# Attention scores q k^T: another order of the 32 KB pieces in the large loads, and of the heads on TensorE

## The chip, the cores and the metric

The kernel runs on one core of a Trainium2 chip. The metric is the device time of one execution in microseconds (us), as the median of several runs. A core has a matrix engine (PE, or TensorE), three engines for elementwise work (DVE or VectorE, ACT or ScalarE, POOL or GpSimd), SP, which here only issues DMAs, and sixteen DMA engines that move data between the memory outside the core (DRAM, here HBM) and the on-chip memory (SBUF, 128 partitions). PE writes into PSUM, a small memory of its own, from which ACT or DVE copies.

## The reference

For each of 8 x 12 = 96 heads the kernel computes the 1024 x 1024 matrix of dot products of the rows of q with the rows of k, over 64 elements, in float32.

```python
batch, n_heads, seq, head_dim = 8, 12, 1024, 64
def reference(q, k):
    return np.einsum('bhid,bhjd->bhij', q, k).astype(np.float32)
```

The inputs are 25.2 MB each, the output is 402.65 MB.

## The kernel before

**Blocks.** The 96 heads are worked in nine blocks of 2, 2, 4, 8 and then five times 16 heads (`sizes`, `NMAX` is 16). For each block, q and k are loaded, cast to fp16, transposed so that the 64 elements of a row lie along partitions, and then multiplied head by head. Two blocks (i and i+1) have their transposed q and k in SBUF at a time (`qk_sb[i % 2]`): block i is multiplied while block i+1 is loaded, cast and transposed. Blocks 0 and 1 go another way (transposed by PE, `cast_rows` and `transpose_rows`), which the change does not touch.

**The load** (`Block.load`, L152 to L164). A block of N heads is one stretch of DRAM. It is cut into 128 equal consecutive pieces, and piece p goes to partition p of `x_sb` as one row. For N = 16 a piece is 32 KB, 128 rows of 64 float32, an eighth of a head, and the load has 4 MB. The 128 partitions are dealt to the sixteen DMA engines, eight to each: by the words of the change, partition 8e+b to engine e as its packet b. So engine e reads the sixteenth of the block that is head e, and at any moment the sixteen engines are 256 KB apart. In block 3 (N = 8) the pieces have 16 KB and the engines are 128 KB apart, in block 2 (N = 4) 8 KB and 64 KB.

There is one raw buffer of 32 KB per partition, so from block 4 on (`i > EARLY`) the load of k waits until q's last cast, and the next q until k's last. The loads of the blocks of 16 are issued from ACT's queue by `next_load(act)`, at heads 1 and 7 of the block before; for block 4 it is head 1 of block 2 and head 2 of block 3 (`LOADS`). All stores are issued from SP's queue.

**Casts and transposes.** `cast_quads` (L200, casts at L210) runs on POOL: it takes a chunk of 32 partitions of raw float32 and writes it as fp16 into one quadrant of a half buffer. Four casts make one chunk, of which each block of 16 has eight: q or k, part 0 or 1, and two halves of the rows (`chunks`). Part 0 takes the partitions 0 to 31 and 64 to 95, part 1 the others, so that in the half buffer the lower 64 partitions hold the two halves of 32 elements of each row from raw partitions below 64, and the upper 64 those from above. `transpose_quads` (L221 to L235) then has DVE transpose the chunk in squares of 32 x 32, which puts the 64 elements of a row along 64 partitions, and its output pattern puts each row at its place in the head. Heads whose raw rows lay in partitions 0 to 63 end in the lower 64 partitions of `qk`, that is in the lower half of PE's rows, the others in the upper half. There are three half buffers. The eight chunks of block i+1 are transposed at the heads `TURNS` of block i, or spread evenly in the first blocks.

**The scores** (`Block.scores`, L255). For head n, `half` says in which half of PE it lies and `g` at which place there. Each head has eight weight loads (L308) and sixteen matmuls of 512 columns (L311). ACT copies PSUM to one of three output buffers (`o_sb`, L288), and SP stores each finished head with one DMA of 4 MB (L301): row 8p+t of the head comes from partition p, so each partition's 32 KB are consecutive in DRAM, and each DMA engine writes 256 KB in a row. Heads are stored in their own order.

**What sets the order of work.** The order on each engine is written out by hand: the loop in `block` calls `scores` for each head, and inside it, after the first or second group of matmuls of a head, the transposes and loads that are due at that head. Head 0 of a block waits for all transposes of the block (`self.ready`); the first copy of a head waits until the store three heads before has left its buffer.

## Time and profile before

| | |
|---|---|
| Runs of the kernel before, median (lowest to highest of 3) | 1062.69 us (1061.64 to 1063.31) |
| The profiled execution | 1062.84 us |
| its span, first to last instruction | 1061.0 us |
| granted TensorE clock | 1.000 |
| busy PE, ACT, DVE, POOL | 700.2, 697.1, 431.0, 354.2 us |
| moved by DMA | 453.21 MB, 427 GB/s over the span |
| HBM read, written | 50.33 MB, 402.65 MB |
| a store of 4 MB, issue to landing, median of 96 | 21.8 us |
| a load of 4 MB, issue to landing, median of five of q, five of k | 24.1, 24.3 us |

How to read it: the profile is of one execution, taken on the chip. "Busy" is the time in which an engine worked. The page cuts the span into 40 slices; its DMA row gives the busy share of the sixteen DMA engines in tenths, 9 standing for 90% or more, and the row below it the rate. For each DMA queue it gives packets, megabytes, and the time of the packets as a share of sixteen engines over the span; since packets overlap a little at their ends, a share over a short window can exceed 100%. A group row gives line, engine, operation, output and input, how many, then busy time, mean ns of one, and the idle time of the engine just before them with what ended most of it. A row for one line gives the shortest, median and longest duration in ns instead. The chain is the work that ended last, followed back step by step to what released it; its rows are start, length, and what ran. Beside its views, the trace holds a record of each DMA packet: start, length, bytes and queue, but not which of the sixteen engines moved it.

### The profile page before, as it was taken

To read this page: it belongs to the slowest core of one execution; us is meant where nothing else is said; L and a number is where in the kernel's file an instruction comes from. 1 tells how busy PE (TensorE), PEld (TensorE's weight loads), DVE (VectorE), ACT (ScalarE), POOL (GpSimd) and SP (SyncE) were. 2 spreads that over 40 slices of the span, in tenths; PEclk is the share of its full clock that TensorE was granted. 3 is DMA by queue.
4 is the path that set the end of the run, shared out by engine and by line. 5 is a ranking of instruction groups with operands and counts; after the bars stand their busy time and mean duration, and the time that the engine had idled before them with its cause. 6 is when DMAs were issued, how large, how long until landed. Compare 5 with 4: busy or idle time off the path is not lost.

```text
span 1061.0 us, 3307 instructions
## 1 busy us (share of the span) xinstructions
PE 700.2 (66%) x1568; PEld 127.3 (12%) x800; DVE 431.0 (41%) x55; ACT 697.1 (66%) x386; POOL 354.2 (33%) x206
## 2 busy tenths in 40 slices
PE   6876744957477748567765856775584777778770
PEld 1111100111011101011111101111110111111110
DVE  2995939029193009339003907600761920000000
ACT  4766655857477747567756756775675777777771
POOL 7927465056380028064006509100913700000000
DMA  9999999999999999999999999999999999999997
GB/s 376 434 435 435 434 434 434 416 421 432 431 434 434 435 429 428 426 435 432 432 422 434 435 427 433 433 434 423 433 429 432 435 434 431 434 434 431 432 431 322
DMA packets 17009, 453.21 MB, mean 427 GB/s; under 512 B 1888, under 2 KB 1888, under 8 KB 2912
## 3 DMA queue, kind: packets, MB, share of 16 engines
q1 hardware_dynamic: 14976, 410.00, 89.7%
q10 hardware_dynamic: 2016, 42.99, 9.8%
q8 instruction: 9, 0.15, 0.0%
q14 instruction: 8, 0.07, 0.0%
HBM read 50.33 MB, written 402.65 MB: 427 GB/s over the span
## 4 chain that ended last, share of the span: by engine, by line
DMA 65%; ACT 16%; PE 7%; DVE 5%; POOL 4%; issue 1%; ACTq 0%; SPq 0%
DMA out_dram<-o_sb 60%; ACT o_sb L288 16%; PE ps_all L311 7%; DVE kT L229 4%; POOL half L210 3%; DMA x_sb<-in_k_dram 2%; DMA x_sb<-in_q_dram 2%; DVE qT L229 1%; DMA o_sb<-in_q_dram 0%; PE ps_all L243 0%; POOL qT L181 0%; DVE kT L250 0%; ACT kT L250 0%; ACTq L36 0%; SPq L169 0%
## 5 line engine op out<-in xcount | busy, mean ns | idle before, releaser
L288 ACT COPY o_sb<-ps_all 128x2048 f32<-128x2048 f32 (+1 forms) x384 | 694.8, 1859 | 333.5 <-DMA out_dram<-o_sb 290.2
L311 PE MATMUL ps_all<-kT,qT 64*128 64x512 f16 x1536 | 696.1, 617 | 328.6 <-ACT o_sb L288 312.8
L210 POOL CAST half<-x_sb 32x2048 f16<-32x2048 f32 x176 | 332.3, 1888 | 482.1 <-DMA x_sb<-in_q_dram 302.2
L229 DVE STREAM_TRANSPOSE qT<-half 128x2048 f16<-128x2048 f16 x22 | 202.6, 9478 | 268.1 <-POOL half L210 268.1
L229 DVE STREAM_TRANSPOSE kT<-half 128x2048 f16<-128x2048 f16 x22 | 202.5, 9539 | 137.5 <-POOL half L210 137.5
L308 PEld LDWEIGHTS <-qT 64*128 64x128 f16 x768 | 124.2, 162 | 897.4 <-issue 878.0
L229 DVE STREAM_TRANSPOSE kT<-kT 128x1024 f16<-128x1024 f16 x2 | 9.4, 4870 | 0.0
L229 DVE STREAM_TRANSPOSE qT<-qT 128x1024 f16<-128x1024 f16 x2 | 9.2, 4780 | 0.0
L210 POOL CAST qT<-o_sb 32x1024 f16<-32x1024 f32 x8 | 8.3, 1035 | 1.2 <-DMA o_sb<-in_q_dram 0.8
L210 POOL CAST kT<-o_sb 32x1024 f16<-32x1024 f32 x8 | 8.3, 1035 | 0.5
L250 DVE COPY qT<-ps_all 128x1024 f16<-128x1024 f16 x2 | 2.4, 1224 | 11.1 <-PE ps_all L243 11.1
L288 DVE COPY o_sb<-ps_all 128x1024 f32<-128x1024 f32 x4 | 4.9, 1225 | 4.4 <-PE ps_all L311 4.4
L243 PE MATMUL ps_all<-ident,qT 128*128 128x128 f16 x16 | 2.1, 311 | 6.8 <-POOL qT L181 6.7
L250 ACT COPY kT<-ps_all 128x1024 f16<-128x1024 f16 x1 | 1.0, 1012 | 4.8 <-PE ps_all L243 4.8
L181 POOL CAST qT<-o_sb 128x512 f16<-128x512 f32 x4 | 2.3, 615 | 3.7 <-DMA o_sb<-in_q_dram 3.7
L250 ACT ACT_TABLE_LOAD x1 | 1.3, 1283 | 2.8 <-issue 2.8
L250 DVE COPY kT<-ps_all 128x1024 f16<-128x1024 f16 x1 | 1.2, 1225 | 4.4 <-PE ps_all L243 4.4
L243 PE MATMUL ps_all<-ident,kT 128*128 128x128 f16 x16 | 2.0, 305 | 0.7 <-ACT o_sb L288 0.7
L181 POOL CAST kT<-o_sb 128x512 f16<-128x512 f32 x4 | 2.4, 618 | 0.3 <-DMA o_sb<-in_q_dram 0.3
L243 PEld LDWEIGHTS ps_all<-ident,qT 128*128 128x128 f16 x16 | 1.5, 141 | 7.1 <-POOL qT L181 7.1
L243 PEld LDWEIGHTS ps_all<-ident,kT 128*128 128x128 f16 x16 | 1.5, 136 | 3.3 <-POOL qT L210 1.6
L359 POOL MEMSET ident<- 128x128 f16 x1 | 0.2, 205 | 0.5 <-SPq L98 0.5
(5 smaller groups left out, 0.7 us busy)
## 6 DMA issues: line engine op xcount, KB each, us to landing
out_dram<-o_sb SPq DMA_DIRECT2D x96, 4096.0 KB, 21.8
x_sb<-in_q_dram ACTq DMA_DIRECT2D x5, 4096.0 KB, 24.1
x_sb<-in_k_dram ACTq DMA_DIRECT2D x5, 4096.0 KB, 24.3
x_sb<-in_q_dram SPq DMA_DIRECT2D x1, 2048.0 KB, 14.6
x_sb<-in_k_dram SPq DMA_DIRECT2D x1, 2048.0 KB, 19.5
o_sb<-in_k_dram ACTq DMA_DIRECT2D x4, 256.0 KB, 4.8
o_sb<-in_q_dram SPq DMA_DIRECT2D x4, 256.0 KB, 5.1
o_sb<-in_q_dram SPq DMA_DIRECT2D x1, 1024.0 KB, 8.2
```

Source lines behind the costliest of these rows:

```text
L181: lambda: nc.gpsimd.tensor_copy(out=rows[:, :, h], in_=self.raw[x][:, h * n : (h + 1) * n].rearrange("p (r d) -> p r d", d=D),),
L210: lambda: nc.gpsimd.tensor_copy(out=dst[q0 : q0 + 32].rearrange("p (r d) -> p r d", d=32), in_=raw[32 * b : 32 * b + 32, c * m : (c + 1) * ...
L229: lambda: nc.vector.transpose(out=dst, in_=buf.rearrange("p (r i) -> p r i", i=32)),
L243: lambda: nc.tensor.transpose(t_ps[:, t], rows[:, t], ident),
L250: lambda: copy(out=dst, in_=t_ps.rearrange("c t m -> c m t")), [done]
L288: lambda: (nc.vector.tensor_copy if by_dve else nc.scalar.copy)(out=dst, in_=ps[:, : w * S]),
L308: return nc.tensor.ldweights(stationary, tile_position=(at, 0))
L311: return nc.tensor.add_instruction(mybir.InstMatmult(name=nc.get_next_instruction_name(), ins=[nc.tensor.lower_ap(moving), nc.tensor.lower ...
L359: cleared = gps.run(lambda: nc.gpsimd.memset(ident, 0.0))
```

## The change

The five blocks of 16 heads (`spread`) are cut into the same 128 pieces of 32 KB, but partition 8e+b now receives piece 16b+e, where it received piece 8e+b. So packet b of the sixteen engines covers 512 KB in a row, two heads. A head's eight pieces are now in eight engines' packets of one number b: head 2b lies in the partitions with e below 8, that is 0 to 63, and head 2b+1 in the upper ones. Therefore the output pattern of the DVE transpose places column e and b separately (it has one more dimension), and in `scores` even heads lie in the lower, odd heads in the upper half of PE, where the first eight heads lay in the lower and the last eight in the upper half. Loads of the smaller blocks, stores, casts, copies and the order of instructions on each engine and queue stay.

```diff
+            self.spread = N == NMAX
...
-            dma = eng.eng.dma_start(
-                out=self.raw[x], in_=src.rearrange("(p r) d -> p (r d)", p=P)
-            )
+            if self.spread:
+                src = src.rearrange("(b e r) d -> e b (r d)", b=NT, e=P // NT)
+            else:
+                src = src.rearrange("(p r) d -> p (r d)", p=P)
+            dma = eng.eng.dma_start(out=self.raw[x], in_=src)
...
-            dst = self.qk[x][:, part * n : (part + 1) * n].rearrange(
-                "c (i r) -> c r i", i=32
-            )[:, c * m : (c + 1) * m]
+            if self.spread:
+                dst = self.qk[x].rearrange("c (b q e r) -> c q r e b", b=NT, q=2, e=4)
+                dst = dst[:, part, c * m : (c + 1) * m]
+                src = buf.rearrange("p (r e b) -> p r e b", e=4, b=NT)
+            else:
+                dst = self.qk[x][:, part * n : (part + 1) * n]
+                dst = dst.rearrange("c (i r) -> c r i", i=32)[:, c * m : (c + 1) * m]
+                src = buf.rearrange("p (r i) -> p r i", i=32)
...
-                lambda: nc.vector.transpose(
-                    out=dst, in_=buf.rearrange("p (r i) -> p r i", i=32)
-                ),
+                lambda: nc.vector.transpose(out=dst, in_=src),
...
-            half, g = divmod(n, self.N // 2)
+            if self.spread:
+                g, half = divmod(n, 2)
+            else:
+                half, g = divmod(n, self.N // 2)
```

## The prediction

> **What bounds the kernel now.** I read the page first: slices, DMA queues, chain, groups.

> ```profile
> DMA  9999999999999999999999999999999999999997
> GB/s 376 434 435 435 434 434 434 416 421 432 431 434 434 435 429 428 426 435 432 432 422 434 435 427 433 433 434 423 433 429 432 435 434 431 434 434 431 432 431 322
> ...
> q1 hardware_dynamic: 14976, 410.00, 89.7%
> q10 hardware_dynamic: 2016, 42.99, 9.8%
> ...
> DMA out_dram<-o_sb 60%; ACT o_sb L288 16%; PE ps_all L311 7%; DVE kT L229 4%; POOL half L210 3%; DMA x_sb<-in_k_dram 2%; DMA x_sb<-in_q_dram 2%; DVE qT L229 1%; DMA o_sb<-in_q_dram 0%; PE ps_all L243 0%; POOL qT L181 0%; DVE kT L250 0%; ACT kT L250 0%; ACTq L36 0%; SPq L169 0%
> ...
> L288 ACT COPY o_sb<-ps_all 128x2048 f32<-128x2048 f32 (+1 forms) x384 | 694.8, 1859 | 333.5 <-DMA out_dram<-o_sb 290.2
> L311 PE MATMUL ps_all<-kT,qT 64*128 64x512 f16 x1536 | 696.1, 617 | 328.6 <-ACT o_sb L288 312.8
> L229 DVE STREAM_TRANSPOSE kT<-half 128x2048 f16<-128x2048 f16 x22 | 202.5, 9539 | 137.5 <-POOL half L210 137.5
> ```

> The DMA engines are never free. ACT idles 290.2 us for o_sb to be stored, PE idles 312.8 us for ACT, and the sum of engine idle time in the trace's DMA packet records, between 5 and 1050 us, is 0.09 us per engine. So the end is a sum of packet times, and a faster compute engine buys nothing. Queue q1 holds the stores, q10 the loads. The dips in GB/s (416, 421, 422, 423) fall in slices with a big load.

> The load packets cost a little more per byte. q1: 0.897 x 1061.0 x 16 / 410.00 = 37.1 us of one engine per MB; q10: 0.098 x 1061.0 x 16 / 42.99 = 38.7. The difference, 1.56 x 42.99 / 16, is 4.2 us per engine. The packet records are sharper: the 1280 32 KB packets of the ten big loads last 1.2536 us in the mean against a median of 1.213, so 80 packets per engine x 0.0406 = **3.25 us**. That is all that a better read order can win in the mean.

> Next, where it is lost: the DMA view of two 4 us windows in the load that runs from 201.8 to 222.5 us, first 206 to 210, then 212 to 216 (packets, MB, share of 16 engines).

> ```profile
> q1 hardware_dynamic: 27, 0.88, 51.2%
> q10 hardware_dynamic: 24, 0.79, 45.5%
> ```

> ```profile
> q10 hardware_dynamic: 31, 1.02, 74.0%
> q1 hardware_dynamic: 30, 0.56, 32.4%
> ```

> In the first, half of the engines read and half write: 0.455 x 64 / 24 = 1.213 us a load packet. In the second, one store has run out, the next has just begun, most engines read at once, and a load packet takes 0.740 x 64 / 31 = 1.53 us. The records show the same in six other big loads: up to 2.3 us a packet in one to four microseconds around the handover of two stores, 1.213 elsewhere. Sixteen engines reading at once are not slow as such: from 13.0 to 16.6 us nothing but block 3's load runs, whose engines stand 128 KB apart (8 pieces of 16 KB):

> ```profile
> q1 hardware_dynamic: 97, 1.57, 102.5%
> ```

> 1.025 x 57.6 / 96 = 0.615 us for 16 KB (one of the 97 is a semaphore write); the fastest such packet took 0.611. The big loads stand 256 KB apart.

> **The change, part by part.** No instruction is added, removed or moved: five loads of q and five of k (the four smaller ones on SP's queue stay as they are), the same 160 big casts and 40 transposes of the five 16-head blocks, the same order on every engine and queue.

> *The read order.* At any moment the sixteen engines now read neighbouring 32 KB pieces, 512 KB in a row, instead of sixteen places 256 KB apart. The packets keep their 32 KB and their partitions, so nothing changes on the SBUF side. The trace has no packet at 32 KB pitch. Bounds from the nearest rows: the 128 KB row (0.615 against 0.611, 0.6%) leaves 80 x 1.213 x 0.006 = 0.6 us of the 3.25; the first load's 1.213 leaves nothing; the worst load's mean (1.3125 us, that of 201.8 us) would cost 80 x (1.3125 - 1.2536) = 4.7 us more than now. I take the 128 KB row, as the only one with sixteen readers and no writer, so the bursts go.

> [...]

> But not the mean engine ends the kernel. Each store ends with one 4-byte semaphore packet per engine; the median of the last sixteen starts at 1054.28 us, the last at 1059.28. One engine falls behind by 0.069 us per store in the 74 store intervals without a big load (the median engine by 0.002). So I count on the last landing. Over the ten stretches of 2 or 3 stores with a load, it took 3.38 us more than its packets at 1.2103 us each (their start-to-start time in undisturbed stretches); the median engine 3.69. Of the 3.38, the same drift in the 21 stores is 1.45 and, if reads drift too, in 80 load packets 0.69. So the gain on the path lies between 1.24 and 3.38 us. The ends are about equally far from what the rows say, since the last engine need not be the same one throughout; I take the middle, **-2.3 us**.

> *The transposes.* The output pattern becomes four-dimensional: 64 by 4 by 8 elements, with steps of 256 and 2048 bytes where one run of 32 had 256.

> ```profile
> L229 DVE STREAM_TRANSPOSE qT<-half x22: 9323/9512/9561, 46.1 to 777.4; 128x2048 f16<-128x2048 f16 x22
> L229 DVE STREAM_TRANSPOSE kT<-half x22: 9311/9588/9689, 64.5 to 846.7; 128x2048 f16<-128x2048 f16 x22
> L229 DVE STREAM_TRANSPOSE qT<-qT x2: 4695/4780/4865, 28.3 to 32.6; 128x1024 f16<-128x1024 f16 x2
> ```

> These rows hold steps of 64 bytes (the 1024-element form), 128 and 256, all at 4.6 to 4.7 ns per element; so I take no change. It could be dearer: no row has two inner steps. The cover is thin in one place, the chain of waits from 118 to 188 us:

> ```profile
> 118.08 23.96 DMA x_sb<-in_k_dram
> ...
> 149.85 36.75 DVE kT L229 x4
> 186.60 0.05 issue
> 186.65 1.94 PE ps_all L311 x4
> ```

> Block 4's k load, four casts, four transposes, then PE and ACT, and the store of head 16 is issued at 196.08, when the fastest engine runs out of stores at 197.2. So at most 1.1 us of delay is hidden there, 0.28 us or 3% per transpose; what is above that goes to the end four times over. The later blocks end their transposes (at 327.6 us the first) tens of microseconds before they are used.

> *The head order.* 80 heads alternate between the halves of PE. If each lost the overlap of its first weight load, 80 x 0.16 us = 13 us would lie on PE, inside the 312.8 us it waits for ACT. A longer issue of the loads on ACT's queue (0.33 us now; SP's took 0.50) would be 10 x 0.17 = 1.7 us under ACT's 290.2. Both nothing.

> **Sum.** The profiled execution took 1062.84 us, its span 1061.0 and 1.84 around it. 1062.84 - 2.3 = 1060.5; the median of the runs is 0.15 lower, so **1060.4 us**. About 0.2%, 2.1 us, is what a measurement of this kernel can tell from no change; the forecast stands at that edge.

> **Rivals.**
> 1. *The bursts belong to the handover, not to the pitch*: most engines read at once and wait for the same thing at any pitch. For it: the last two rounds of block 3's loads, at 21.3 us, took 0.87 us a packet at 128 KB pitch, and the first big load none at 256. Against: the clean 13.0 to 20 us. 1062.7, no change.
> [...]
> 3. *Slower: the 512 KB window collides in itself.* Neighbouring pieces at equal offsets are read by all sixteen at once; place: the handovers of all ten loads. At the worst load's mean, 1062.7 + 4.7 = 1067.4; it decides from a mean load packet above 1.254 us. Against it: 64 KB pitch (block 2's load, 8 KB packets) cost 0.314 us against 0.309, 1.7%.
> 4. *Slower: the four-dimensional transposes.* At 10% more: 4 x 0.95 - 1.1 = 2.7 us, 1065.4; doubled, 4 x 9.5 - 1.1 = 37 us, 1100. Decides from 3%. Against it: three steps at one price.

> **Chances.** Forecast 0.56, within 1059.0 to 1061.6; 0.41 of it beyond 2.1 us, 0.15 within. Rival 1 0.13, rival 2 0.07 (counted as no change), rival 3 0.14, rival 4 0.10. Faster is 0.41 and a hundredth for what the list leaves out, same 0.15 + 0.13 + 0.07 less that hundredth, slower 0.24. The range runs from 1058.6 (all 4.2 us of the page's difference gone) to 1066.0, which takes in the near half of rivals 3 and 4.

> **What would show it.** q10 at 9.4 to 9.5% of the engines, no window with load packets over 1.25 us, L229 at 9.3 to 9.7 us, the last landing some 2 us earlier with the same spread of 5 us between engines. [...] A drift of the last engine that itself depends on where the loads read would make the gain larger than counted.

## The result, and the profile after

| | before | after |
|---|---|---|
| median of 4 runs each | 1062.62 us (1061.64 to 1063.31) | 1123.92 us (1122.30 to 1128.39) |
| ratio, 95% interval | | 1.0584 (1.0553 to 1.0616) |
| the profiled execution | 1062.84 us | 1124.31 us |
| 32 KB load packets, mean of 1280 | 1.2536 us | 1.8628 us |
| 32 KB store packets, mean of 12288 | 1.2148 us | 1.2290 us |
| idle time per DMA engine, from 5 us to the end of the first engine to finish | 0.1 us | 1.1 us |

The kernel is 61 us slower; the forecast was 2 us faster. The page of the changed kernel, the rows that answer to those of before:

```profile
GB/s 378 437 355 399 394 362 433 387 356 432 333 430 438 431 332 425 419 376 430 436 409 343 433 377 398 431 436 380 412 434 340 432 430 436 434 429 436 430 434 313
...
q1 hardware_dynamic: 14976, 410.00, 85.8%
q10 hardware_dynamic: 2016, 42.99, 13.5%
...
L297 ACT COPY o_sb<-ps_all 128x2048 f32<-128x2048 f32 (+1 forms) x384 | 694.9, 1859 | 395.0 <-DMA out_dram<-o_sb 350.0
L237 DVE STREAM_TRANSPOSE kT<-half 128x2048 f16<-128x2048 f16 x22 | 202.1, 9468 | 166.3 <-POOL half L213 166.3
...
x_sb<-in_q_dram ACTq DMA_DIRECT2D x5, 4096.0 KB, 31.6
x_sb<-in_k_dram ACTq DMA_DIRECT2D x5, 4096.0 KB, 30.8
```

Packets and bytes are the same to the last digit, the time of q10 is not: 0.135 x 1122.5 x 16 / 42.99 = 56.4 us of one engine per MB, where it was 38.7. The rate falls to between 332 and 425 GB/s in the slices that hold a big load or a good part of one, and stands at 429 to 438 elsewhere, but for the first and the last slice. Compute is as it was, ACT only waits longer for stores (350.0 us, before 290.2), and the transposes cost what they did. In the kernel before, the packets of the first of the ten loads took 1.213 us each from its start to its end. The DMA view of 70 to 74 us, in that load, first in the kernel before, then in the changed one (packets, MB, share of 16 engines):

```profile
q10 hardware_dynamic: 31, 1.02, 58.8%
q1 hardware_dynamic: 23, 0.75, 43.6%
```

```profile
q10 hardware_dynamic: 16, 0.52, 49.9%
q1 hardware_dynamic: 22, 0.72, 46.6%
```

Before, 0.588 x 64 / 31 = 1.21 us a load packet; now 0.499 x 64 / 16 = 2.00 us a load packet and 0.466 x 64 / 22 = 1.36 us a store packet: both queues suffer, the reads most, and not only at handovers but through the whole load, whose packets take 1.957 us in the mean. Per engine the terms are 80 load packets x 0.6092 = 48.7 us, 768 store packets x 0.0142 = 10.9, idle 1.0: 60.6 of the 61.5 us between the two profiled executions.

### The profile page after: what moved, and what is told of

Read it like the earlier page. It is cut to its first block, busy times and chain, and to the rows that moved or that the text cites. A ratio compares the mean times of both kernels' runs of the same rounds, so it can differ in the third digit from the quotient of the medians.

```text
span 1122.5 us, 3307 instructions
## 1 busy us (share of the span) xinstructions
PE 700.6 (62%) x1568; PEld 125.7 (11%) x800; DVE 430.2 (38%) x55; ACT 697.2 (62%) x386; POOL 354.4 (32%) x206
## 2 busy tenths in 40 slices
DMA  9999999999999999999999999999999999999997
## 3 DMA queue, kind: packets, MB, share of 16 engines
q1 hardware_dynamic: 14976, 410.00, 85.8%
q10 hardware_dynamic: 2016, 42.99, 13.5%
## 4 chain that ended last, share of the span: by engine, by line
DMA 67%; ACT 15%; PE 7%; DVE 5%; POOL 3%; issue 1%; ACTq 0%; SPq 0%
DMA out_dram<-o_sb 61%; ACT o_sb L297 15%; PE ps_all L320 7%; DVE kT L237 4%; POOL half L213 3%; DMA x_sb<-in_q_dram 3%; DMA x_sb<-in_k_dram 3%; DVE qT L237 1%; DMA o_sb<-in_q_dram 0%; PE ps_all L249 0%; POOL qT L184 0%; DVE kT L256 0%; ACT kT L256 0%; ACTq L36 0%; SPq L172 0%
## 5 line engine op out<-in xcount | busy, mean ns | idle before, releaser
L297 ACT COPY o_sb<-ps_all 128x2048 f32<-128x2048 f32 (+1 forms) x384 | 694.9, 1859 | 395.0 <-DMA out_dram<-o_sb 350.0
L256 DVE COPY qT<-ps_all 128x1024 f16<-128x1024 f16 x2 | 2.5, 1225 | 10.9 <-PE ps_all L249 10.9
```

Source lines behind the costliest of these rows:

```text
L256: lambda: copy(out=dst, in_=t_ps.rearrange("c t m -> c m t")), [done]
L297: lambda: (nc.vector.tensor_copy if by_dve else nc.scalar.copy)(out=dst, in_=ps[:, : w * S]),
```

## The experiments

**Which part.** The new read order on the old kernel, and the changed kernel with the old read order:

```diff
-                out=self.raw[x], in_=src.rearrange("(p r) d -> p (r d)", p=P)
+            if self.N == NMAX:
+                src = src.rearrange("(b e r) d -> e b (r d)", b=NT, e=P // NT)
```

> The kernel before with the new read order of the ten large loads alone; transposes and head order stay, so the output holds the rows of a block in another order. If the read order is the whole cause, about 1124 us (61 us over the kernel before), load packets at 1.86 us in the mean where they were 1.25. If the four-dimensional transposes or the alternating halves of PE carry part of it, clearly less, below 1110.

> The changed kernel with the old read order; four-dimensional transposes and alternating halves stay, so the output holds the rows of a block in another order. If the read order is the whole cause, 1062 to 1063 us, no change against before, transposes at 9.5 us. If the other two parts cost anything, above 1065.

Measured: the order alone 1124.14 us, ratio 1.0590 (1.0565 to 1.0615), load packets at 1.858 us; the rest alone 1063.62 us, a little above the expected 1063, ratio 1.0008 (0.9998 to 1.0017), load packets at 1.261 us. The DMA queues of the two, first the order alone, then the rest alone:

```profile
q10 hardware_dynamic: 2016, 42.99, 13.5%
```

```profile
q10 hardware_dynamic: 2016, 42.99, 9.8%
```

The read order is the whole cause. The alternating halves and the four-dimensional transposes cost nothing that can be measured: by the interval, at most 1.8 us.

**Is it the distance?** Single loads ahead of the kernel, first alone, then beside two stores, with every distance between neighbouring engines that could matter:

```diff
+    for pitch, kind in PATTERNS:
+        sp.wait(filled)
+        filled = [probe_in.start(nc.sync.dma_start(out=x_sb, in_=pieces(pitch, kind)))]
```

> The kernel before, preceded by single 4 MB loads of 128 packets of 32 KB, thirteen patterns, each first alone and then beside two stores: distance between neighbouring DMA engines 256 KB (as before), 32 KB (as after), 33, 34, 36, 40, 48, 64, 128, 512 KB, 1 MB, and the first two again. Theory A (engines that read at equal offsets of a distance of exactly 32 KB meet in the same part of the memory): 32 KB at 1.6 us a packet or more even alone, 33 to 40 KB back at 1.21 to 1.3. Theory B (512 KB in a row hold too little of the memory's width): 33 to 40 KB as slow as 32, 64 KB about halfway, 128 KB at 1.22. Theory C (the reads only lose against the stores beside them): every pattern 1.21 to 1.25 alone, and 32 KB at 1.86 beside stores only.

Measured, from the packet records (mean us of a 32 KB packet):

```
distance      256 KB  32    33    34    36    40    48    64    128   512   1 MB  256   32
alone         1.29    2.47  2.48  2.46  2.43  2.47  2.47  2.47  2.50  2.49  2.50  1.28  2.46
beside stores 1.22    2.02  2.03  2.03  1.81  2.00  1.88  1.96  1.91  1.86  1.83  1.22  1.95
```

All three theories fell. Every distance but 256 KB is slow, 33 KB (2.48 us) as 32 (2.47) and 1 MB (2.50) as 32, by the same factor of about two against 1.29, and without any store. The DMA view of two of the loads alone, 8.8 to 19.8 us (256 KB), then 43.7 to 64.2 us (33 KB):

```profile
DMA packets 144, 4.19 MB, mean 381 GB/s; under 512 B 16, under 2 KB 16, under 8 KB 16
```

```profile
DMA packets 144, 4.19 MB, mean 205 GB/s; under 512 B 16, under 2 KB 16, under 8 KB 16
```

What sets 256 KB apart is not the place: its pieces lie in a row, so its source can be written as a plain list of 128 rows just as well, and it ran like one (1.29 us), while all the others are sixteen by eight (sixteen groups of eight pieces; 16 is the outermost number of the source) and took 2.43 us or more. So a new theory, D: a source of sixteen by eight is dealt to the DMA engines in another way, eight neighbouring partitions to each, and then engines meet on the side of SBUF.

**The deal.** Loads one at a time; and the whole kernel with the old places, bytes and partitions, but each load issued as eight loads of sixteen partitions eight apart, with a control of eight loads by columns:

```diff
+                lanes = self.raw[x].rearrange("(e b) n -> b e n", b=NT)
+                far = src.rearrange("(e b r) d -> b e (r d)", b=NT, e=16)
+                parts = [(lanes[b], far[b]) for b in range(NT)]
```

> The kernel before, preceded by loads one at a time, nothing beside them. Theory D (the new pattern gives each DMA engine eight neighbouring partitions, and then two engines write into the same group of SBUF partitions at once, each at half speed): 128 x 32 KB contiguous 1.21 to 1.3 us a packet; 128 partitions from places 33 KB apart, two dimensions, also 1.21 to 1.3; three dimensions with 128 outermost (two 16 KB runs each) 0.61 to 0.66 a 16 KB packet; sixteen by eight 2.4 to 2.5; eight loads of sixteen partitions eight apart 2.4 to 2.5, from the new places and from the old ones alike; eight loads of sixteen neighbouring partitions 4.8; four loads of 32 neighbours and two of 64 2.4. [...] Theory E (a source with three dimensions, or one that is not contiguous, is slow in itself): the 33 KB places or the two-run load at twice the time, and the loads of sixteen partitions eight apart, which have two dimensions each, at 1.21. Theory B again (the place in DRAM): old places 1.21, new places 2.4.

> The kernel before, each of the ten large loads issued as eight loads of sixteen partitions eight apart, so that partition 8e+b still receives piece 8e+b: same bytes, same places, same output, only dealt to the DMA engines as after. Theory D: 1115 to 1130 us, load packets at 1.8 to 1.9 us. Theories B and E: 1062 to 1066 us.

> The control for the former: each large load issued as eight loads of 128 partitions and 4 KB columns, dealt as before. All theories: 1062 to 1070 us (small packets may cost 2% of 97 us, 2 us); if eight DMAs in place of one cost much by themselves, above 1075.

Measured in the probe (packet records, mean us; 32 KB packets but for the third row):

```
128 partitions, contiguous                               1.30
128 partitions, places 33 KB apart, two dimensions       1.28
128 partitions x two runs of 16 KB, three dimensions     0.65
sixteen by eight                                         2.49
eight loads of 16 partitions 8 apart, new places         2.45
eight loads of 16 partitions 8 apart, old places         2.49
eight loads of 16 neighbouring partitions                4.36
four loads of 32, two of 64 neighbouring partitions      2.50, 2.48
```

The DMA view of the second, fourth, sixth and seventh row (14.1 to 25, 39 to 60.3, 84 to 105 and 106.5 to 142.3 us); the third and fourth of these count 112 more semaphore packets:

```profile
DMA packets 144, 4.19 MB, mean 385 GB/s; under 512 B 16, under 2 KB 16, under 8 KB 16
```

```profile
DMA packets 144, 4.19 MB, mean 197 GB/s; under 512 B 16, under 2 KB 16, under 8 KB 16
```

```profile
DMA packets 256, 4.19 MB, mean 200 GB/s; under 512 B 128, under 2 KB 128, under 8 KB 128
```

```profile
DMA packets 256, 4.19 MB, mean 117 GB/s; under 512 B 128, under 2 KB 128, under 8 KB 128
```

Neither gaps (1.28 us) nor a third dimension (2 x 0.65) cost anything against 1.30 while 128 is the outermost number on both sides; two dimensions are slow when the sixteen packets in flight go to partitions eight apart (2.45); old places are as slow as new ones (2.49); and sixteen neighbours are slower still, 117 GB/s. That is D on every row (the neighbours 4.36 where 4.8 was expected), and excludes the place in DRAM (B) and the shape of the source as such (E). The probe's last loads, two single packets into partitions 0 and s with s from 1 to 96, decided nothing: the first packet after a pause took 1.89 to 2.63 us into partitions 1 to 3 apart and 1.83 to 2.38 us into the others.

In the whole kernel, old places with the new deal took 1113.18 us, ratio 1.0489 (1.0454 to 1.0524), load packets at 1.740 us: a little below the expected 1115 and 1.8, far from 1066. In its profiled execution, the slowest of its four (1120.67 us), load packets make 80 x 0.4867 = 38.9 us, stores 768 x 0.0120 = 9.2 and idle time 5.7, of 57.8 in all. So the old places with another deal bring most of the 61 us, not all. Its loads run otherwise, too: nine of the ten have 180 to 235 store packets among their 128, where the changed kernel has 105 to 114, so fewer load packets are in flight at once. Whether that is all of the difference of 11 us was not tried.

The control failed for a reason of its own: 1208.06 us, ratio 1.1366 (1.1347 to 1.1384), though its 4 KB packets took 0.170 us (1.36 per 32 KB). Its waits show why:

```profile
POOL half L220 <- DMA x_sb<-in_q_dram: 506.4, 5, 128.4
...
ACT o_sb L298 <- issue: 262.5, 10, 56.0
```

The packets of the two queues went about in turn (from 411.6 to 494.6 us, 1024 load packets beside 938 store packets), so 4 KB load packets beside 32 KB store packets got 4.2 of 34.9 MB; q lands up to 81.3 us after its issue (before 24.1 in the median), ACT stands with k's load in hand (its wait is for POOL's casts of q) and makes no output meanwhile, and the DMA engines are idle for 141 us each. It says nothing on D; that eight DMAs in place of one do no harm by themselves rests on the probe, where sixteen by eight as one load and as eight cost the same (2.49 and 2.45 us).

**Which partitions meet.** Deeper queues, so that the first packet weighs less: four loads in a row, n packets into n partitions s apart.

```diff
+    for n, s in ((16, 7), (16, 8), (16, 4), (16, 2), (16, 1), (16, 5), (2, 4), (2, 32), (2, 1), (2, 64)):
+        last = (n - 1) * s + 1
+        steps.append([(t[0:last:s], pieces[i, :n]) for i, t in enumerate(tiles)])
```

> The kernel before, preceded by transfers one kind at a time, nothing beside them. First ten kinds of load, each four loads in a row of n packets of 32 KB into n partitions s apart (four buffers, so four packets per DMA engine). [...] Then a load of 128 partitions, then stores: contiguous 1.21, 128 partitions to places 36 KB apart 1.21, sixteen by eight 2.4 if reading SBUF clashes as writing does, 1.21 if it does not.

> As the probe before: loads of n packets into n partitions s apart, four in a row, one kind at a time. [...]

Measured (median us of a packet; us from the first packet's start to the last one's end, for the four loads):

```
2 partitions:   4 apart 1.21, 5.7   8: 1.25, 5.6   16: 1.21, 5.7   64: 1.21, 5.8   96: 1.21, 5.9
                1 apart 2.56, 10.3  32: 2.57, 10.3  35: 2.41, 9.5
4 partitions:   4 apart 1.21, 5.8   7: 1.21, 5.9   32: 2.53, 10.1
8 partitions:   4 apart 1.53, 6.5   7: 1.41, 9.4 (8 of 32 packets above 2.1)   8: 2.56, 10.0   16: 2.56, 10.2
16 partitions:  8 apart 2.56, 10.2  4: 2.56, 10.3  2: 2.55, 10.3  1: 4.82, 18.7  7: 2.48, 9.7  5: 2.52, 10.0
stores of 128:  contiguous and spaced 1.22, 16 x 8: 2.51
```

The DMA view of two partitions 4 apart (91.3 to 97.2 us) and 32 apart (98.7 to 109.2):

```profile
DMA packets 16, 0.26 MB, mean 44 GB/s; under 512 B 8, under 2 KB 8, under 8 KB 8
```

```profile
DMA packets 16, 0.26 MB, mean 25 GB/s; under 512 B 8, under 2 KB 8, under 8 KB 8
```

Two packets at once into partitions 0 and 32, 0 and 1 or 0 and 35 went at half speed (2.41 to 2.57 us), into 0 and 4, 8, 16, 64 or 96 at full speed (1.21 to 1.25); of eight partitions 7 apart 8 of 32 packets were slow and two chains of them ended 2.9 us after the rest, as one slow pair (0 and 35) would have it, so engines did not hold each other up there. The other loads of 4 and 8 partitions fit the pairs: slow at 8, 16 and 32 apart (2.53 to 2.56 us), where partitions 32 apart are among them, and not slow at 4 and 7 apart with four partitions (1.21). Eight partitions 4 apart, without any of the slow pairs among them, took 1.53 us; why is not shown. Two rows do not fit: 16 partitions 7 apart begin with the same eight, of which 24 of 32 packets had not been slow, and here all were (2.48 us), as were those 5 apart (2.52). Why is open; it was not tried further. So the clash is shown for pairs. With sixteen packets in flight, every spacing took 2.48 to 2.56 us but that of neighbours, 4.82, and these rows leave a rival: that sixteen engines go at half speed with any deal but that of a plain list of 128, which by itself does not give the neighbours' 4.82. Stores of sixteen by eight are slow too (2.51 us against 1.22), so transfers out of SBUF were slowed as those into it were.

**The price per load.** The new order on k's five loads alone (`and x == 1` added to the first diff):

> The new read order on the five loads of k alone, q as before; transposes and head order as before, so the output is not the reference's. If the cost is a price per load packet, half of the 61 us: 1091 to 1096 us. If it only appears once a load is late for the next block (a stall), much less than half or all of it.

Measured: 1094.05 us, ratio 1.0291 (1.0264 to 1.0318). Half of the loads, half of the cost: 31.3 of 61. It is a price per packet, not a stall: load packets (1.861 us in k's loads, 1.238 in q's, 1.550 in the mean of both) make 80 x 0.2962 = 23.7 us, stores 5.8, idle time 2.2.

## Why the prediction was wrong

The step that failed is the sentence "The packets keep their 32 KB and their partitions, so nothing changes on the SBUF side", and under it the deal that I took over from the words of the change, partition 8e+b on engine e both before and after. Each partition still gets one packet of 32 KB; what changes, by the rates, is which engine writes it. Before, source and destination were both lists of 128, and the packets ran as if the sixteen in flight never met: 1.213 us in the median. Had that load been dealt 8e+b, engines 0 and 4, for one, would have written into partitions 32 apart at the same time, and it would have run at the 2.45 to 2.49 us that sixteen partitions eight apart cost in the probe. After, the source's outermost number is sixteen, and the load runs like that deal: 2.49 us alone, 1.863 in the kernel. The step thus put at nothing measured 48.7 us in the load packets and 10.9 in the stores beside them. That the read order is the cause is shown, and so is that the place in DRAM is not needed for it; which engine holds which partition is not in any record and is inferred from these rates.

Point by point:
- *What bounds the kernel* was right, and so was the way to count: the sum of packet and idle times per engine gives 60.6 of 61.5 us. This is also why the full price shows: no engine had time to spare.
- *The read order*: the bounds, from 3.25 us less to 4.7 us more, came from rows at other distances in DRAM. All of these rows were lists of 128 partitions, and none could show the other side. With 128 outermost, a distance of 33 KB between pieces cost nothing visible: 1.28 us, contiguous ones 1.30. Whether the new order with the old deal would have taken the bursts away remains open; it was not tried.
- *The transposes*: right, 9.3 to 9.6 us again, with steps of 256 and 2048 bytes. *The head order and the issue*: right, nothing.
- *The gain of 2.3 us on the last engine*: never came to be. Nor is the spread between the engines at the end smaller: 9.8 us (1111.0 to 1120.7), before 5.8.
- *Rival 2* is in the chances with 0.07, as no change. No run shows the deal it was priced for, since no record names the engine that moved a packet; what the runs showed is a loss, 48.7 us per engine in the load packets. None of the rivals asked whether the deal stays when the source is rearranged. A clash priced in every pair, at the factor of about two that the probes show (2.57 us against 1.21), would have come to 80 x 1.213 = 97 us more as the upper end. The kernel lost less per packet than that, 0.609 us; that the other engine of a pair is often at a store packet may be why, but it was not tried.
- *Rival 3* had the right loads and the right sign and the wrong mechanism: it expected 4.7 us at the handovers of two stores, and 59.6 were lost through the whole of each load. *Rival 4* did not happen.

## What to carry to other kernels

## What the runs showed of the hardware that was not expected

- Sixteen packets into sixteen neighbouring partitions ran at 4.36 to 4.51 us each in the mean, 3.6 to 3.7 times a packet's 1.213, and 117 GB/s for the load.
- In the changed kernel the stores slowed too, to 1.36 us in the window shown, though their own pattern is as before. Why is not shown.
- Two queues shared the DMA engines packet by packet, not byte by byte: loads in packets an eighth of the size (1024 of them beside 938 store packets) landed up to 81.3 us after issue, and the kernel took 145 us longer.
- The first 32 KB packets after a pause were slow with nothing beside them, in contiguous loads too: in six of them the first sixteen took 1.8 to 2.0 us in the median and up to 2.35, the later ones 1.21.
